# Four-pass output projection, half of the sample attention beside projections, plain first products and paired scores in a two-layer encoder step

## The chip, the cores and the metric

The kernel runs on one core of a Trainium2 chip, in one launch. The metric is the time of one execution on the device in microseconds. The engines are TensorE (matmuls, in the profile PE, its weight loads PEld), VectorE (DVE), ScalarE (ACT), GpSimd (POOL), and SyncE (SP), which issues most of the transfers.

## The reference

One inference step of two layers, d_model 1024, on 512 prompt tokens (one sequence) and 128 sample tokens (8 sequences of 16 new tokens, each with 512 cached keys and values).

- Layer 0: RMSNorm; a projection into mixer A (8 heads of 64, stick-breaking attention, strictly causal) and mixer B (gated linear attention, 4 heads); both outputs side by side through one output projection; residual.
- Layer 1: RMSNorm; mixer C, 16 heads of 64, softmax over 64-token chunks and the eight chunks before, with a learned bias by distance; output projection; residual.
- After each mixer RMSNorm and a SwiGLU FFN (hidden 2816), residual; a last RMSNorm.

```python
xp = xp + _ab_merge(oa, ob, r, norm_gla_g[i], w_out_ab[i])      # cat(oa, ob) @ w_out
...
xp = xp + (oc.reshape(Bp, Tp, C_WIDTH) @ w_out_c[i])
...
def _swiglu(h, wg, wu, wd):
    return (jax.nn.silu(h @ wg) * (h @ wu)) @ wd
```

Outputs are the normed tokens of both groups and the new keys, values and states.

## The kernel before

All 640 tokens are five blocks of 128 (four prompt blocks, one sample block). Every fp32 weight and activation that goes through a large matmul is split into a high and a low fp32r part (`split`: a ScalarE cast, L273, and a VectorE subtraction, L274), and each product is three matmuls (high-high, high-low, low-high). Weights come through `load_raw` (L267) on SyncE's queue into two buffers.

Order. The kernel is written against a tile framework that places instructions by a simulated timeline: an instruction goes when its inputs and buffers are there, lowest priority number first. Program order gives the number unless `priority(...)` sets one; the mixers' attention has large negative numbers and so is put in as soon as it can go, with projections filling in. Each engine, and each queue of transfers, then runs its own list in order.

Layer 0 (to about 447 us): `ORDER` lists the projections (V values, P query/key pair, G, K, R for mixer B, M its recurrence). `proj_ws` (L288 to L290) keeps the weight stationary, 320 tokens at a time; `proj_as2` (L337 to L340) gives values. After each pair `attend_prompt` runs the two heads of the pair: for each query block b and each head, three matmuls of contraction length 64 (rows 0 to 63 for head 0, 64 to 127 for head 1) put scores into a bank of PSUM (`za`), L436 to L438; `weights` turns them into weights (stick-breaking L403 to L411, softmax L418 to L423); transposes (L444) go back into the same bank, copies to SBUF follow (L447, L449), and the value products (L455) land in head 0's bank.

`attend_sample` does one of the eight sample sequences with all 8 heads of a half (a step): it loads the values (`vr`, 1 MB, L481, two buffers that it shares with the prompt's value tiles) and the keys (`kr`, four of 256 KB, L486), transposes the keys (L489), makes scores (L496), weights, their transposes (L508, L510), value products (L517) and a last transpose (L521). Mixer A has 8 steps, mixer C 16 (two halves).

`mixer_end` closes a mixer. It splits the outputs into `oH` and `oL` (L538, L539), issues all sample steps, then `out_prompt` (L561 to L563; four stretches of 256 output columns over the four prompt blocks, with the norm of each block in the last stretch; `WHEN` gives their place among the sample's priorities), and at the end `out_sample` (L579 to L581), which loads and splits the weight again for the sample block and normalises it.

FFN (`ffn`): the token operand is cut into quadrants b11, b12, b21, b22 (rows of d_model by 320-token halves), and a pair of 128-column weight blocks is multiplied by it with seven products instead of eight (`fast_pair`, L653 to L655) of sums and differences; the weight sums are made by POOL (L659), the token combinations t1 to t4 by VectorE (L621, split by L612 and L613), all at the start of the FFN in `operand`. A down projection (`proj_as`, L307 to L309) follows for each group of hidden blocks (`GROUPS`).

PSUM has eight banks: three for projections (`pp`), and in the mixers `BANKS = ((3, 2), (4, 1))`, that is `za` and `zb` with 3 and 2 in layer 0, 4 and 1 in layer 1; in the FFN all five are one pool.

Of the kernel before, what the change touches and what calls it, by code (L numbers as in the profile page):

```python
# [8 lines left out]
F32 = mybir.dt.float32  # L9
# [31 lines left out]
NGT = 6  # L41
NHL = 4
TAIL = 4
ORDER = "V0 P0 G0 P1 K0 V1 M0 P2 K1 R0 M1 R2 P3 R1 R3"
MPRI = 50000
WHEN = ((20, 20, 20, 20), (4, 8, 12, 15))
BANKS = ((3, 2), (4, 1))
KTA = "bbbb"
KTC = "baba"
# [6 lines left out]
def kernel(  # L56
# [16 lines left out]
    @contextmanager  # L73
    def mixer_pools(na, nb):

        with tc.tile_pool(name="mix", bufs=1, reuse_waits="tile") as m:
            pools["stage"] = m
            with tc.tile_pool(name="pza", bufs=na, space=PSUM, reuse_waits="tile") as a:
                with tc.tile_pool(name="pzb", bufs=nb, space=PSUM, reuse_waits="tile") as b:
                    banks.update(za=a, zb=b)  # L80
                    yield

    @contextmanager
    def ffn_pools():
        with tc.tile_pool(name="ffn", bufs=1, reuse_waits="tile") as m:
            pools["stage"] = m
            with tc.tile_pool(name="pf", bufs=5, space=PSUM, reuse_waits="tile") as a:
                banks.update(za=a, zb=a)
# [13 lines left out]
    qk = tagged("qk", NQK)  # L102
# [13 lines left out]
    def za(shape, name="za"):  # L116
        return banks["za"].tile(shape, F32, tag="za", name=name)
# [115 lines left out]
    def norm_block(xt, gi, hT, b, sb=None, bank=None):  # L233
        r = rstd_of(xt, sb)
        for i in range(2):
            tp = (bank or za)([P, 4, P], "tp")
# [59 lines left out]
    def proj_as(l, W, c0, n, lhs, evac, tail=1):  # L296
# [3 lines left out]
        ps = [pp([P, n], "pn") for _ in range(3)] + [za([P, n], "pn") for _ in range(2)]  # L300
# [73 lines left out]
    def evac_k(dst, kfd, kout_p, kout_s, hp):  # L374

        def f(ps):
# [8 lines left out]
            with priority(2 * FIRST):  # L385
                tp = zb([P, 4, P], "ktp")
# [3 lines left out]
                tp2 = zb([P, P], "ktp2")  # L390
# [35 lines left out]
    def attend_prompt(qT, kT, v, c0, odst, weights, mask):  # L426


        for b in range(4):
            n = (b + 1) * P  # L430
            bs = slice(b * P, n)
            wTs, zs = [], []
            for h in range(2):
                z = za([P, 512], "z")
                r = slice(64 * h, 64 * h + 64)
                MM(z[:, :n], lhsT=qT[r, 0, bs], rhs=kT[r, 0, :n], start=True, stop=False)  # L436
                MM(z[:, :n], lhsT=qT[r, 0, bs], rhs=kT[r, 1, :n], start=False, stop=False)
                MM(z[:, :n], lhsT=qT[r, 1, bs], rhs=kT[r, 0, :n], start=False, stop=not mask)  # L438
                if mask:
                    MM(z[:, bs], lhsT=identb, rhs=mask_a, start=False, stop=True)  # L440
                w = weights(h, n, z[:, :n])
                wT = vr_([P, b + 1, P], "wT")
                for j in range(b + 1):
                    nc.tensor.transpose(z[:, j * P:(j + 1) * P], w[:, j * P:(j + 1) * P], ident)  # L444
                zv = z[:, :n].rearrange("p (j t) -> p j t", t=P)
                if h == 0:
                    nc.scalar.copy(wT, zv)  # L447
# [720 lines left out]
```

## Time and profile before

| | |
|---|---|
| median of 3 runs | 1823.07 us (1819.52 to 1823.08) |
| profiled execution | 1823.8 us, span of its instructions 1822.1 us |
| TensorE busy | 1732.9 us (95%), mean granted clock 0.969 |
| VectorE, ScalarE, GpSimd busy | 1142.8, 833.8, 327.7 us |
| HBM | 175.75 MB read, 14.29 MB written |

A matmul's row in the time order gives its start and its own time; matmuls overlap, so the cost of one is the distance between starts. Rows by tile give smallest, median and largest time in ns and the starts of the first and the last. The granted clock (PEclk) is the share of full speed that TensorE was allowed.

### The profile page before, as it was taken

The page shows a single profiled execution, that of the slowest core. Times are in us where ns is not written, and L with a number is a line of the kernel's source. Part 1 is how long each engine was busy: PE and PEld are TensorE (multiplying, and loading weights), DVE is VectorE, ACT ScalarE, POOL GpSimd, SP SyncE. Part 2 cuts the span into 40 slices and gives each one's busy share as a digit, 9 for nine tenths or more (in the row PEclk, how much of TensorE's full clock was granted, in tenths as well). Part 3 has the DMA queues.
Part 4 walks back from the last instruction along what each step waited for, and adds up shares of the span by engine and source line. Part 5 has one row for each costly group of instructions (what it writes and reads, how often), then busy time and mean ns, then how long its engine had stood idle before and what let it go on. Part 6 is the DMA issues. An engine that isn't in the chain of part 4 may idle for free.

```text
span 1822.1 us, 31879 instructions
## 1 busy us (share of the span) xinstructions
PE 1732.9 (95%) x12504; PEld 1550.1 (85%) x12504; DVE 1142.8 (63%) x2285; ACT 833.8 (46%) x1837; POOL 327.7 (18%) x355
## 2 busy tenths in 40 slices
PE   8999998998899999999799999999878999999997
PEld 7898986976898989989698888888757989999896
DVE  5466576767964846747635554665658747658475
ACT  6453444556642534525424333444545525435253
POOL 2000000002513413222200000000104314133130
PEclk9998997998999999999799999999988999999999
DMA  5311222573222232221342223257862222312212
GB/s 141 94 56 47 66 83 95 179 255 105 70 93 70 75 100 63 100 74 66 110 128 77 80 89 95 85 178 263 278 214 65 81 81 72 103 58 93 93 59 81
DMA packets 157430, 192.10 MB, mean 105 GB/s; under 512 B 13232, under 2 KB 109504, under 8 KB 157280
## 3 DMA queue, kind: packets, MB, share of 16 engines
q1 hardware_dynamic: 153696, 178.40, 30.4%
q0 software_dynamic: 3584, 11.67, 2.0%
q8 instruction: 98, 1.61, 0.4%
q14 instruction: 52, 0.43, 0.1%
HBM read 175.75 MB, written 14.29 MB: 104 GB/s over the span
## 4 chain that ended last, share of the span: by engine, by line
PE 80%; DVE 12%; DMA 4%; ACT 2%; issue 2%; SPq 0%; DVEq 0%; ACTq 0%
PE pn L307 6%; PE pn L309 5%; PE pn L308 5%; PE pw L288 5%; PE pw L289 5%; PE pw L290 5%; DVE wl L274 4%; PE px L653 3%; PE px L654 3%; PE px L655 3%; PE z L455 3%; PE py L655 3%; DMA kr<-in_cache_c_k_dram 2%; PE pm L337 2%; PE py L653 2%; PE py L654 2%
## 5 line engine op out<-in xcount | busy, mean ns | idle before, releaser
L274 DVE TENSOR_TENSOR wl<-raw,wh 128x512 fp32r<-128x512 f32 (+1 forms) x350 | 279.3, 807 | 220.8 <-ACT wh L273 218.7
L273 ACT CAST wh<-raw 128x512 fp32r<-128x512 f32 (+1 forms) x350 | 215.4, 618 | 347.3 <-PE pn L309 162.6
L659 POOL TENSOR_TENSOR sw<-raw 128x512 f32<-128x512 f32 x88 | 121.6, 1386 | 498.9 <-DMA raw<-in_w_ffn_gate_dram 292.9
L273 ACT CAST wh<-sw 128x512 fp32r<-128x512 f32 x176 | 109.3, 621 | 177.8 <-PE px L654 78.2
L274 DVE TENSOR_TENSOR wl<-sw,wh 128x512 fp32r<-128x512 f32 x176 | 139.7, 798 | 60.3 <-ACT wh L273 49.1
L308 PE MATMUL pn<-wl,gT 128*128 128x512 f32 x440 | 172.7, 393 | 0.0
L309 PE MATMUL pn<-wh,gT 128*128 128x512 f32 x440 | 170.7, 392 | 0.0
L307 PE MATMUL pn<-wh,gT 128*128 128x512 f32 x440 | 168.8, 394 | 0.0
L655 PE MATMUL py<-xb,wl 128*128 128x320 f32 x352 | 113.1, 321 | 8.4 <-DVE wl L274 8.2
L653 PE MATMUL py<-xb,wh 128*128 128x320 f32 x352 | 111.4, 316 | 6.1 <-ACT wh L273 4.6
L654 PE MATMUL pq<-xt,wh 128*128 128x320 f32 x352 | 109.1, 310 | 2.9 <-DVE xt L613 2.7
L654 PE MATMUL px<-xt,wh 128*128 128x320 f32 x352 | 109.7, 312 | 1.6 <-DVE xt L613 1.6
L654 PE MATMUL py<-xb,wh 128*128 128x320 f32 x352 | 110.7, 314 | 0.0
L653 PE MATMUL px<-xt,wh 128*128 128x320 f32 x352 | 109.5, 311 | 0.0
L655 PE MATMUL px<-xt,wl 128*128 128x320 f32 x352 | 109.4, 311 | 0.0
L653 PE MATMUL pq<-xt,wh 128*128 128x320 f32 x352 | 109.1, 310 | 0.1
L655 PE MATMUL pq<-xt,wl 128*128 128x320 f32 x352 | 108.6, 309 | 0.0
L309 PEld LDWEIGHTS pn<-wh,gT 128*128 128x128 f32 x440 | 83.5, 190 | 17.4
L308 PEld LDWEIGHTS pn<-wl,gT 128*128 128x128 f32 x440 | 83.6, 190 | 17.2
L307 PEld LDWEIGHTS pn<-wh,gT 128*128 128x128 f32 x440 | 83.4, 190 | 16.8
L288 PE MATMUL pw<-hTa,wh 128*128 128x320 f32 (+1 forms) x272 | 89.5, 329 | 0.0
L290 PE MATMUL pw<-hTa,wl 128*128 128x320 f32 (+1 forms) x272 | 88.7, 326 | 0.0
(331 smaller groups left out, 4778.3 us busy)
## 6 DMA issues: line engine op xcount, KB each, us to landing
raw<-in_w_ffn_gate_dram SPq DMA_DIRECT2D x44, 512.0 KB, 4.1
raw<-in_w_ffn_up_dram SPq DMA_DIRECT2D x44, 512.0 KB, 3.7
raw<-in_w_ffn_down_dram SPq DMA_DIRECT2D x44, 512.0 KB, 3.3
kr<-in_cache_c_k_dram SPq DMA_DIRECT2D x64, 256.0 KB, 4.8
vr<-in_cache_c_v_dram SPq DMA_DIRECT2D x16, 1024.0 KB, 6.7
raw<-in_w_in_ab_dram SPq DMA_DIRECT2D x24, 512.0 KB, 3.8
raw<-in_w_qkv_c_dram SPq DMA_DIRECT2D x24, 512.0 KB, 3.8
vr<-in_cache_a_v_dram SPq DMA_DIRECT2D x8, 1024.0 KB, 5.5
```

Source lines behind the costliest of these rows:

```text
L273: nc.scalar.copy(H, rawv)
L274: nc.vector.tensor_sub(L, rawv, H.bitcast(F32))
L288: MM(ps[i], lhsT=H[:, k % 4, :], rhs=hT[k][:, 0, s], start=(k == 0), stop=False)
L289: MM(ps[i], lhsT=H[:, k % 4, :], rhs=hT[k][:, 1, s], start=False, stop=False)
L290: MM(ps[i], lhsT=L[:, k % 4, :], rhs=hT[k][:, 0, s], start=False, stop=(k == 7))
L307: MM(ps[b], lhsT=lhs[k][:, 0, bs], rhs=H, start=(k == 0), stop=False)
L308: MM(ps[b], lhsT=lhs[k][:, 0, bs], rhs=L, start=False, stop=False)
L309: MM(ps[b], lhsT=lhs[k][:, 1, bs], rhs=H, start=False, stop=(k == K - 1))
L653: MM(ps, lhsT=H[:, k, :], rhs=X[x][0][k], start=(first and k == 0), stop=False, **f)
L654: MM(ps, lhsT=H[:, k, :], rhs=X[x][1][k], start=False, stop=False, **f)
L655: MM(ps, lhsT=L[:, k, :], rhs=X[x][0][k], start=False, stop=(k == 3), **f)
L659: nc.gpsimd.tensor_tensor(t, a, b, op=op)
```

## The change

Four things, and what they need:

1. `attend_prompt` puts both heads' scores in one tile of two banks (`zz`, one buffer) and issues the six matmuls with the heads in turn; weights are transposed into another bank (`zt`: one buffer in layer 0, two in layer 1), and the value products land in head 1's transpose bank. `zb` has two and one. Key transposes, norms and sample steps take their banks from `zt`, `zb` and `zz`.
2. `out_prompt` and `out_sample` give way to `out_pass`: all five blocks, one half of the 8 input chunks (`kh`) by one half of the output columns (`half`), 512 columns a matmul, added to the residual rows after each pass. A mixer ends with four passes, mixer A with kh 1 (mixer B's outputs) first, mixer C with kh 0 first.
3. Mixer C's sample steps of half 0 are issued two at a time after the attention of pairs 4 to 7, with priorities between them; those of half 1 in `mixer_end`. Mixer A's are in `mixer_end`, four before the first pass and four after.
4. In the FFN the first weight pair is multiplied with eight plain products; the combinations t1 to t4 are written after the first products of the next two weight pairs.

The residual rows move into the large tile pool (18 buffers), query and key tiles into the mixers' pool, some FFN operands into the gate pool (9 buffers, 6 before).

```diff
+BANKS = ((1, 2), (2, 1))
...
+    def zz(name="zz"):
+        t = banks["zz"].tile([P, 2, 512], F32, tag="zz", name=name)
+        return [t[:, 0, :], t[:, 1, :]]
...
+            zs = zz("z")
+            for i, j in ((0, 0), (0, 1), (1, 0)):
+                for h in range(2):
+                    r = slice(64 * h, 64 * h + 64)
+                    MM(zs[h][:, :n], lhsT=qT[r, i, bs], rhs=kT[r, j, :n], start=(i + j == 0),
+                       stop=(i == 1 and not mask))
...
+            ws_ = [weights(h, n, zs[h][:, :n]) for h in range(2)]
+            wTs, ts = [], []
+            for h, w in enumerate(ws_):
+                t = zt([P, 512], "wtp")
...
-            o = zs[0][:, :P]
+            o = ts[1][:, :P]
...
+    def out_pass(W, kh, half, x, done=None):
+        HL = []
+        for k0 in (4 * kh, 4 * kh + 2):
+            raw = load_raw(W[k0 * P:(k0 + 2) * P, 512 * half:512 * half + 512], 2, 512)
+            for i in range(2):
+                HL.append(split(raw[:, i:i + 1, :], 1, 512))
+        for b in range(NB):
+            bs = slice(b * P, (b + 1) * P)
+            ps = pp([P, 512], "po")
+            for i in range(4):
...
+                MM(ps, lhsT=oHc, rhs=H, start=(i == 0), stop=False)
+                MM(ps, lhsT=oHc, rhs=L, start=False, stop=False)
+                MM(ps, lhsT=oLc, rhs=H, start=False, stop=(i == 3))
+            nc.vector.tensor_add(x[b][half], x[b][half], ps)
+            if done is not None:
+                done(b)
...
+        for st in sample[:4]:
+            st()
+        halves(k0)
+        x = [load_x(xsrc(b)) for b in range(NB)]
+        out_pass(W, k0, 0, x)
+        for st in sample[4:]:
+            st()
+        out_pass(W, k0, 1, x)
+        halves(1 - k0)
+        out_pass(W, 1 - k0, 0, x)
+        out_pass(W, 1 - k0, 1, x, lambda b: norm_block(x[b], gi, hT, b))
...
+        def plain():
+            HL = []
+            def part(n):
+                if n == 0:
+                    HL.extend([split(A[m][k], 4, P) for k in range(2)] for m in range(2))
+                for m in range(2):
+                    ps = zb([P, 320], "pb")
+                    for k in range(2):
+                        product(ps, None, (("b11", "b21"), ("b12", "b22"))[n][k], k == 0, HL[m][k])
+                    out(m, n, ps, None)
+            return part
...
+                    part = whole()
+                    block("b11")
+                    block("b21")
+                    part(0)
+                    block("b12", gt_)
+                    block("b22")
+                    part(1)
+                    mats[1][0]()
+                    mats[2][0]()
+                    comb("t3", "b22", "b12")
+                    block("t3")
+                    comb("t1", "b12", "b11")
+                    comb("t2", "b22", "t1")
+                    block("t2")
+                    block("t1")
+                    comb("t4", "b21", "t2")
+                    block("t4", gt_)
+                    continue
...
+    def c_steps(half):
...
+            if half == 0:
+                z.append(zt([P, 512], "zs"))
+            elif not z:
+                z.extend(zz("zs"))
+            p = FIRST + 200000 + (40000 + 5000 * b + 5500 if half == 0 else 90000 + 1000 * b)
...
+            with priority(p):
+                attend_sample(cache_c_k, cache_c_v, b, cs, qbd[half], zn, vt4[:, cs],
...
+                              oS[:, 4 * half:4 * half + 4, :], z.pop(0), "bbbb" if half == 0 else "baba")
...
+        for p in range(p0, p0 + 4):
+            if p > p0:
+                c_attend(p, *c_pair(p))
+            for st in steps[2 * (p - p0):2 * (p - p0) + 2]:
+                st()
+        steps = c_steps(half)
...
-    xt = mixer_end(w_out_c[0], oT, oS, lambda b: xd[b], 3, hT, lambda: [c_sample(h) for h in range(2)],
-                   [FIRST + 299500 + 1000 * t for t in WHEN[1]])
+    xt = mixer_end(w_out_c[0], oT, oS, lambda b: xd[b], 3, hT, steps, 0)
```

More of the change, by code (lines that the diff above doesn't have):

```diff
@@ L471, in new_key_scores, with attend_sample @@
         return zn
-    def attend_sample(ck, cv, b, cs, qbd, zn, vnew, weights, oS, kttp):
+    def attend_sample(ck, cv, b, cs, qbd, zn, vnew, weights, oS, z, kttp):
         def rows(src):
@@ new lines, in mixer_end, with halves @@
+    def mixer_end(W, oT, oS, xsrc, gi, hT, sample, k0):
+        for half in (oH, oL):
+            half[:] = [None] * 4
+        def halves(kh):
+            for i in (2 * kh, 2 * kh + 1):
+                oH[i], oL[i] = [t5([P, 2, NT], "oHL", F32R) for _ in range(2)]
+                out_split(oT[i], i, slice(0, SEQ))
+                out_split(oS[:, 2 * i:2 * i + 2, :], i, slice(SEQ, NT))
+        for st in sample[:4]:
[9 more added lines that the diff above has]
+        out_pass(W, 1 - k0, 1, x, lambda b: norm_block(x[b], gi, hT, b))
+        return x
@@ L603, in operand, with comb @@
     def operand(fT):
         n1, n2 = slice(0, 320), slice(320, NT)
-        out = {}
-        def block(nm, srcs):
+        out, t = {}, {}
+        t["b11"] = [fT[kp][:, :, n1] for kp in range(2)]
+        t["b21"] = [fT[2 + kp][:, :, n1] for kp in range(2)]
+        t["b12"] = [fT[kp][:, :, n2] for kp in range(2)]
+        t["b22"] = [fT[2 + kp][:, :, n2] for kp in range(2)]
+        def comb(nm, a, b):
+            t[nm] = []
+            for kp in range(2):
+                x = ws([P, 2, 320], "xs")
+                nc.vector.tensor_sub(x, t[a][kp], t[b][kp])
+                t[nm].append(x)
@@ L695, in tail @@
             out(1, 0, st["Q"], st["U"])
-        return head, body, tail
+        return head, body, tail, plain
     def ffn(l, xt, fT, after):
-        X = operand(fT)
+        X, comb, block = operand(fT)
         c0, silu = 0, []
@@ L703, in ffn @@
             for c in range(c0, c0 + G, 2):
[L704 removed]
+                gt = [gt_([P, 2, NT], "gT", F32R) for _ in range(2)]
                 gT += gt
@@ L726, in ffn @@
                     mats.append(fast_pair(w[l], c * P, X, o))
-            for i, (head, body, tail) in enumerate(mats):
-                if i == 0 or not (gi == 0 and i == 1):
+            for i, (head, body, tail, whole) in enumerate(mats):
+                if gi == 0 and i == 0:
+                    part = whole()
[16 more added lines that the diff above has]
+                    continue
+                if gi or i > 2:
                     head()
-                if gi == 0 and i == 0:
-                    mats[1][0]()
-                if i:
+                if i > (gi == 0):
                     mats[i - 1][2]()
```

222 lines of the change are left out of this document (73 added, 149 removed).

## The prediction

> **What bounds the kernel now.** I read the page's totals first, then the busy time of every engine in stretches of my choosing, then TensorE's instructions in order of time where a term needs a price, then the tables by tile for first and last starts.
>
> ```profile
> span 1822.1 us, 31879 instructions
> PE 1732.9 (95%) x12504; PEld 1550.1 (85%) x12504; DVE 1142.8 (63%) x2285; ACT 833.8 (46%) x1837; POOL 327.7 (18%) x355
> ```
>
> TensorE is busy for 95% of the span and no other engine is above 63%. What that is made of differs by stage:
>
> ```profile
> core 0: us, PE busy (x) PEld busy (x) DVE busy (x) ACT busy (x) POOL busy (x), PEclk, DMA share, GB/s
> 100.00:310.00 210.00, 208.44 (x1442) 181.50 (x1441) 133.66 (x269) 92.53 (x208) 7.15 (x12) 0.94 0.21 63
> 331.70:447.10 115.40, 103.04 (x1127) 88.34 (x1125) 79.31 (x157) 71.25 (x153) 11.37 (x29) 0.96 0.58 197
> 447.00:480.00 33.00, 28.21 (x154) 25.98 (x154) 31.34 (x45) 22.18 (x44) 19.91 (x11) 0.84 0.16 49
> 920.00:1170.00 250.00, 250.00 (x1720) 216.56 (x1720) 130.87 (x414) 93.64 (x244) 13.29 (x25) 1.00 0.29 88
> 1169.70:1369.50 199.80, 176.57 (x2236) 144.64 (x2234) 115.02 (x323) 96.29 (x228) 16.61 (x56) 0.96 0.67 224
> 1208.00:1340.00 132.00, 117.41 (x1747) 100.17 (x1740) 75.84 (x215) 68.04 (x161) 11.98 (x49) 0.99 0.81 270
> 1369.50:1400.00 30.50, 24.68 (x123) 23.34 (x124) 27.66 (x40) 17.41 (x33) 11.12 (x8) 0.78 0.17 53
> ```
>
> Beside projections (100 to 310, 920 to 1170) TensorE has no idle time and the DMA engines stand at 0.21 to 0.29. From 1208 to 1340 it is the other way round: DMA 0.81 at 270 GB/s, TensorE 15 us idle. The two starts of an FFN (447, 1369) have TensorE idle, VectorE nearly full, and a granted clock of 0.84 and 0.78. So instructions taken from TensorE pay in full beside projections; elsewhere it is a chain or a transfer that pays. The stages' ends are these:
>
> ```profile
> L290 PE MATMUL pw<-hTa,wl x272: 302/309/712, 48.9 to 331.7; 128*128 128x320 f32 x128, 128*16 128x320 f32 x8
> L290 PE MATMUL pw<-hTc,wl x256: 302/309/417, 936.3 to 1169.7; 128*128 128x320 f32 x128
> L653 PE MATMUL py<-xb,wh x352: 303/309/636, 447.1 to 1779.3; 128*128 128x320 f32 x176
> ```
> ```profile
> L517 PE MATMUL zs<-vt4c,wT x128: 272/273/421, 1223.9 to 1351.3; 128*32 128x128 f32 x128
> L517 PE MATMUL zs<-vt,wT x64: 272/273/421, 353.5 to 422.9; 128*32 128x128 f32 x64
> ```
>
> Projections end at 331.7 and 1169.7. The samples' last value products run to 422.9 (8 steps, 69.4/7 = 9.9 us apart) and 1351.3 (16 steps, 127.4/15 = 8.5 us apart). The first FFN product comes at 447.1.
>
> **The change. Part 1: two heads' scores in a double bank.** One head's scores at 256 keys:
>
> ```profile
> 1022.51 0.31 PE L289 MATMUL pw<-hTc,wh 128*128 128x320 f32 x1
> 1022.65 0.31 PE L290 MATMUL pw<-hTc,wl 128*128 128x320 f32 x1
> 1022.89 0.38 PE L436 MATMUL z<-kTc,qTc 64*128 64x256 f32 x1
> 1023.11 0.28 PE L437 MATMUL z<-kTc,qTc 64*128 64x256 f32 x1
> 1023.23 0.28 PE L438 MATMUL z<-kTc,qTc 64*128 64x256 f32 x1
> 1023.44 0.42 PE L288 MATMUL pw<-hTc,wh 128*128 128x320 f32 x1
> 1023.69 0.31 PE L289 MATMUL pw<-hTc,wh 128*128 128x320 f32 x1
> ```
> ```profile
> 562.13 0.39 PE L307 MATMUL pn<-wh,gT 128*128 128x512 f32 x1
> 562.36 0.39 PE L308 MATMUL pn<-wl,gT 128*128 128x512 f32 x1
> 562.59 0.39 PE L309 MATMUL pn<-wh,gT 128*128 128x512 f32 x1
> ```
>
> Start to start a matmul costs 0.146 us at 320 columns and 0.228 at 512 (0.46 for two); the line through both gives 0.119 at 256, 0.173 at 384 and 0.065 at 128. From 1022.65 to 1023.69 are 1.04 us, of which two 320s are 0.29: the group costs 0.75, of it 3 x 0.119 columns and 0.39 for entering and leaving the half-height form. Over the four blocks a head costs 3 x (0.065+0.119+0.173+0.228) + 4 x 0.39 = 3.3 us, and a pair 6.6. Afterwards both heads stand in one group, rows 0-63 and 64-127 in turn. No row shows this form; the bounds are the quarter-array products against the half-width ones:
>
> ```profile
> 233.06 1.10 PE L924 MATMUL kv<-vb,kdn 64*64 64x128 f32 x32
> ```
> ```profile
> 1018.03 1.09 PE L455 MATMUL z<-wT,vc 128*64 128x128 f32 x14
> ```
>
> Less the 0.27 us that the last one takes to run out, 32 records in 1.10 us are 27 ns each, 14 in 1.09 are 63: halving the rows as well doubles the rate, so the two halves run side by side. Full overlap gives 3.3 us a pair, a saving of 3.3; none saves only a switch, 1.6; were each change of half to cost 0.2, the pair would lose 2.4. I take 3.0, beside the kv row. Twelve pairs, all where TensorE is full: 12 us in mixer A, 24 in mixer C.
> The Trainium skill (TensorE: Matmul & The Clock Gate, Part 3, Measured speedup) gives four row tiles at once 3.07x, not 4x. At that efficiency two tiles would give 1.54x, a pair 3.8 us, and the saving would be 34 us over twelve pairs rather than the 40 of full overlap; my 36 stands between.
>
> Transposes move from the score bank to another, one bank in A and two in C; they and the value products keep their counts.
>
> **Part 2: four passes.** Per mixer now 384 matmuls of 256 columns and 48 of 512: 384 x 0.119 + 48 x 0.228 = 46 + 11 = 57 us. After: 240 of 512, 54.6. The columns are equal; 2.4 us go. Loads of the weight fall from 24 to 8, splits from 32 to 16; those of the sample's own projection are the ones that stood in a chain. But the last sample value product will be followed by two passes over all blocks, 2 x 60 x 0.228 = 27.3 us, with normalisation of each block behind its last matmul. From the last projection matmul to the FFN's first it takes this now:
>
> ```profile
> 1366.62 0.40 PE L581 MATMUL ps<-wh,oHL 128*128 128x512 f32 x1
> 1369.54 0.41 PE L653 MATMUL py<-xb,wh 128*128 128x320 f32 x1 [2.52 <-ACT wh L273]
> ```
>
> I take these 3 us again and 1.5 for splitting the last outputs: 32 us after the last sample value product, against 24 (422.9 to 447.1) and 18 (1351.3 to 1369.5) now. The passes are full of work where the old tail idled, but the tail itself gets longer.
> Residual rows will land in other tiles, loaded beside a pass; cover gone, one landing, 4 us. Moved tile pools, norm weights and gate buffers issue the same instructions: nothing, or at most 5 us should the two gate tiles kept for the FFN delay a group.
>
> **Part 3: half of the sample beside projections (mixer C).** A step's TensorE cost:
>
> ```profile
> 341.36 0.60 PE L489 MATMUL kttp<-ident,kr 128*128 128x128 f32 x4
> 341.89 0.65 PE L496 MATMUL zs<-kt,qbda 128*32 128x128 f32 x16
> 342.46 0.66 PE L489 MATMUL kttp<-ident,kr 128*128 128x128 f32 x4
> 342.87 0.36 PE L561 MATMUL po<-wh,oHL 128*128 128x256 f32 x1
> ```
> ```profile
> 352.58 1.08 PE L517 MATMUL zs<-vr,wTs 128*32 128x128 f32 x32
> 353.48 0.40 PE L517 MATMUL zs<-vt,wT 128*32 128x128 f32 x8
> 353.81 0.39 PE L561 MATMUL po<-wh,oHL 128*128 128x256 f32 x1
> ```
>
> Half the key side takes 1.51, the values 1.23, six more transposes 0.11 each (four in 0.60, the last 0.27), switches some 0.5 (two of 0.2 to 0.4): 5.4 us. Eight steps are issued along pairs 4 to 7; I let six finish there. They add 32 us where TensorE is full, and pairs 0 to 6 give 21 back: projections end at 1181. The loads (2 MB a step, on SP) find the DMA engines at 0.29; the small copies and clears on POOL queue behind its output issues and the bias clear. A pair here lasts 14 us of projections, some 4.5 of attention and two steps of 5.4, so 15 us a step; the key side, through one bank for its transposes, takes four times 0.7 and a copy of about 0.7, some 6, and the attention chain below another 6 to 8. It just fits, and three pairs give six steps.
>
> ```profile
> L418 DVE CUSTOM_DVE_ANT_0 s<-z,bias 128x128 f32<-128x128 f32 (+3 forms) x64 | 31.2, 490 | 20.2 <-PE z L438 19.2 <-issue 0.6
> L421 ACT ACTIVATE s<-s,m 128x128 f32<-128x128 f32 (+3 forms) x64 | 36.0, 562 | 68.5 <-DVE m L420 68.5
> ```
>
> What remains after 1181: by TensorE the last pair and a half 14, ten steps 54, output 55, norms 4 = 127 us; by the chain four blocks of attention 20 (an estimate: ten steps of about 0.5 us each, as in the two rows above), two late steps 20, seven intervals of 8.5 = 60, then 32: 132 us. The two are nearly equal and share queues, so I add 12: 1181 + 132 + 12 = 1325. Now: 1369.5. **Mixer C: -44 us**, of it 24 by part 1.
>
> **Mixer A.** Projections end 12 earlier, at 320, and the first value product follows at 341. The steps have only two passes as filler (27 us, not 46), so I take 8.7 us an interval instead of 9.9: 341 + 61 + 32 = 434, against 447. **Mixer A: -13**. By TensorE's work alone (43 + 55 + 4 after 320) it would be 422 + 3, -22.
>
> **Part 4: plain products first.** From 447 to 480 stand 146 products and 8 transposes, 22 us of work in 33; from 1369.5 to 1400 115 and 8, 18 in 30.5: 23.5 us lost, waiting for the combined operands and at the lower clock. Now 8 plain products need only uncombined blocks (the first four only three normed token blocks), 14 us, then four heads, 7 us, while the combinations are made. That is 12 matmuls more, 1.75 us each time; three splits and four POOL sums fewer. I leave 4 us lost per start: **-12**. All gone would be -20; cover no better than now +3.5.
>
> **Sum.** This execution took 1823.8 us (span 1822.1 and 1.7 around it), 0.7 above the median of 1823.07. 1823.8 - 44 - 13 - 12 = 1754.8; with 2 of the 5 us at most for the gate tiles, **1757**.
>
> **Rivals.**
>
> ```profile
> L407 DVE TENSOR_TENSOR_SCAN l<-l 128x128 f32<-128x128 f32 (+4 forms) x40 | 36.2, 905 | 0.5
> ```
> ```profile
> SPq L481 <- PE zs L517: 34.8, 19, 5.0
> ```
>
> *The double bank holds the scores back.* There is one, where there were three or four banks; it is free only when both heads have been read. In C that is two reads of 0.49 us, little against 7.8 us of stage per block (250/32); in A the bank stays taken from the first of the stick-breaking steps to the last but one, the scan of 0.9 us and five of about 0.5, the second head's behind the first's: some 6 us of 13 (210/16). If the attention chain and not TensorE then sets the pace, part 1's 36 us do not come: 1793. The Trainium skill (TensorEngine Tiling (Array Packing), Performance Considerations) warns of just this: tiling speeds up TensorE and not the emptying of PSUM. The rows above leave room, so 0.15.
>
> *The half sample is not beside the projections.* The order is a planner's; the value loads have one free buffer of two while the other holds this half's values, and POOL's small steps may be late. If the steps run after the projections after all, mixer C keeps only its 24: 1777, chance 0.12.
>
> *Slower: a value load stops SP's queue.* With one buffer the load of step b+1 waits for step b's products, and the weight loads behind it on SP wait too. Two loaded weights cover 2 x 48 x 0.146 = 14 us of projection; beyond that TensorE stands. To lose all 67 us, eight waits must each exceed 14 + 8.4 = 22 us; at 25 us the time is 1757 + 8 x 11 = 1845. Waits for that buffer now are at most 5.0. Chance 0.09, a third of it with waits that only eat the gain up.
>
> **Chances.** Forecast (1725 to 1775) 0.58, bank 0.15, late steps 0.12, SP 0.09; 0.06 for better than 1725 (TensorE's own sums in both mixers, 1181 + 127 + 3 in C, and clean FFN starts: 22 + 58 + 20 = 100, 1724). 0.2% is 3.6 us, about what this kernel's measurement can tell. Faster 0.91, same 0.03, slower 0.06. Range 1720 to 1800, from the better bounds to just past the bank rival.
>
> **What would show it.** Right: six score matmuls per block within 1.1 us at 512 keys; value loads of the C cache beside projections with DMA above 0.4 there; no long waits for cache keys; first FFN products about 434 and 1306 (1369.5 - 44 - 13 - 6) with the clock at 1.0 soon after. Wrong: TensorE idle beside projections, waiting for weights, or scores waiting for reads; sample steps bunched after the last projection; the passes waiting for the sample's last step.

## The result, and the profile after

The changed kernel takes 1878.8 us (median) against 1821.3 for the kernel before, a ratio of 1.032 (95% interval 1.029 to 1.035): 57 us slower, where 66 less were forecast. Its profiled execution has a span of 1872.1 us, 50 more than the one shown of before. From the page:

```profile
span 1872.1 us, 30990 instructions
PE 1718.5 (92%) x12144; PEld 1510.5 (81%) x12144; DVE 1131.7 (60%) x2247; ACT 815.8 (44%) x1803; POOL 311.9 (17%) x347
```

TensorE does 14 us less work than before and its idle time has grown from 89 to 154 us. Where, the stretches tell (columns as in the prediction: busy time and count of each engine, granted clock, DMA share, GB/s):

```profile
331.00:443.70 112.70, 80.12 (x810) 55.41 (x810) 44.93 (x75) 42.80 (x77) 3.49 (x22) 0.77 0.42 141
443.70:463.40 19.70, 18.70 (x72) 15.10 (x73) 9.97 (x20) 7.14 (x19) 5.92 (x5) 0.85 0.18 54
463.40:480.90 17.50, 8.70 (x43) 5.90 (x41) 15.79 (x42) 14.45 (x44) 4.25 (x5) 0.69 0.18 60
936.00:1181.70 245.70, 245.70 (x2030) 222.42 (x2029) 134.52 (x420) 96.20 (x258) 14.83 (x31) 1.00 0.38 117
1254.00:1389.70 135.70, 103.47 (x1101) 72.45 (x1097) 49.04 (x120) 39.78 (x81) 4.43 (x28) 0.81 0.45 151
1409.20:1426.30 17.10, 8.13 (x42) 6.24 (x41) 14.66 (x42) 14.70 (x44) 4.52 (x4) 0.68 0.18 61
```

Beside mixer C's projections (936 to 1181.7) TensorE is still full. In the samples' stretches (331 to 443.7, 1254 to 1389.7) no engine is: TensorE stands still for 32 us in each, the DMA engines run at 0.42 and 0.45, VectorE and ScalarE are busy for 29 to 40% of the time. Where nothing is full, a chain of dependent instructions is the first thing to look for. The stages' ends by tile (first and last start after "median/max"; the last two rows are the second half of mixer C alone, here and in the kernel before):

```profile
L293 PE MATMUL pw<-hTa,wl x272: 302/309/468, 51.8 to 291.1; 128*128 128x320 f32 x128, 128*16 128x320 f32 x8
L524 PE MATMUL zs<-vt,wT x64: 272/345/421, 353.2 to 442.8; 128*32 128x128 f32 x64
L634 PE MATMUL pb<-xb,wh x64: 307/309/615, 480.9 to 1441.3; 128*128 128x320 f32 x64
L293 PE MATMUL pw<-hTc,wl x256: 302/309/417, 966.3 to 1181.7; 128*128 128x320 f32 x128
L524 PE MATMUL zs<-vt4c,wT x128: 272/273/421, 1142.0 to 1388.8; 128*32 128x128 f32 x128
L524 PE MATMUL zs<-vt4c,wT x64: 272/420/421, 1284.9 to 1388.8; 128*32 128x128 f32 x64
L517 PE MATMUL zs<-vt4c,wT x64: 272/273/421, 1301.7 to 1351.3; 128*32 128x128 f32 x64
```

Mixer A's steps: 89.6/7 = 12.8 us apart (9.9 before). In mixer C the eight steps of the second half take 103.9 us from first to last, 14.8 apart; before, the second half's were 7.1 apart (49.6/7), and 8.5 over all sixteen. The first of these seven intervals is of another kind than the rest: from 1284.9 to 1313.8 TensorE is busy for 28.54 of 28.90 us, since 100 matmuls of output passes stand between the two steps (about 23 us at 0.228 each). The last six take 75.0 us, 12.5 each, with TensorE busy for 48.96 us. The tail, from the last value product to the first FFN product, takes 38.1 us (24.2 before) and, to 1426.3, 37.5 us (18.2). The first FFN starts 33.7 us later than before and lasts 3.8 less; mixer C takes 26.8 more from the first FFN's end to the second's start; the second FFN lasts 6.8 less. Together 49.9, the difference of the spans.

The reason for the 12.5 stands in TensorE's and VectorE's rows in order of time, at the seam of two steps of the second half, where one hands the tile on to the next:

```profile
1314.39 0.29 DVE L527 COPY osb<-zs 128x128 f32<-128x128 f32 x1 [1.18 <-PE zs L524]
1314.73 0.33 PE L528 MATMUL zs<-ident,osb 128*128 128x128 f32 x1 [0.48 <-DVE osb L527]
1315.10 0.46 DVE L532 COPY oSc<-zs 64x64 f32<-64x64 f32 x2 [0.42 <-PE zs L528]
1315.70 0.65 PE L503 MATMUL zs<-kt,qbdc 128*32 128x128 f32 x16 [0.64 <-DVE oSc L532]
```

The last read of one step's tile (L532) ends at 1315.56, and only then do the scores of the next step begin (L503, released by it). All six seams from here on are like this: the scores begin 0.05 or 0.06 us after the last read where the step takes the other bank of the same tile, and 0.15 us after it where the tile is taken anew. In this stretch two steps are never under way together. Before they were: scores of a third step stand at 341.89 and the first step's value products only at 352.58 and 353.48 (rows in the prediction).

Mixer A shows the same with a comparison built in, since its steps take the two halves of the double tile and one bank more in turn. From value product to value product it takes 18.1, 11.0, 8.7, 16.5, 11.1, 8.7 and 15.4 us: the three long intervals are the three at which a step takes the second half of a double tile whose first half the step before it is using.

The waits of 1254 to 1389.7 (total, times, longest) show the cost on ScalarE:

```profile
ACT kt L501 <- PE zs L503: 37.6, 7, 12.7
```

Seven times ScalarE waits, up to 12.7 us, to copy the next step's transposed keys: their buffers are held until the late scores have used them.

The paired scores themselves do what they should. At 512 keys, between projections:

```profile
999.70 0.31 PE L293 MATMUL pw<-hTc,wl 128*128 128x320 f32 x1
999.93 0.96 PE L441 MATMUL z<-kTc,qTc 64*128 64x512 f32 x6
1000.83 0.42 PE L291 MATMUL pw<-hTc,wh 128*128 128x320 f32 x1
1001.08 0.31 PE L292 MATMUL pw<-hTc,wh 128*128 128x320 f32 x1
```

From 999.70 to 1001.08 are 1.38 us, 0.29 of it two projection matmuls: 1.09 for both heads. One head alone cost as much before (1037.97 to 1039.35):

```profile
1037.97 0.31 PE L288 MATMUL pw<-hTc,wh 128*128 128x320 f32 x1
1038.21 0.49 PE L436 MATMUL z<-kTc,qTc 64*128 64x512 f32 x1
...
1039.10 0.42 PE L289 MATMUL pw<-hTc,wh 128*128 128x320 f32 x1
1039.35 0.31 PE L290 MATMUL pw<-hTc,wl 128*128 128x320 f32 x1
```

In mixer A the prompt's own blocks meet the double tile too. There the last read of a block's scores (L413) comes at the end of a long chain of stick-breaking steps:

```profile
238.69 0.96 PE L441 MATMUL z<-kT,qT 64*128 64x512 f32 x6
253.38 0.68 DVE L413 TENSOR_TENSOR l<-z,l 128x512 f32<-128x512 f32 x1
257.08 0.33 PE L441 MATMUL z<-kT,qT 64*128 64x128 f32 x2
```

In the last eight blocks the tile is held for 10 to 18 us and blocks follow 12 to 18 us apart. Projections end 40 us earlier than before (291.1 against 331.7), but the prompt's last value products stand at 331.7, against 328.9.

The tail in mixer A, from the last output matmul to the FFN's first product (rows between left out):

```profile
463.42 0.39 PE L563 MATMUL po<-wh,oHL 128*128 128x512 f32 x1
...
480.10 1.12 PE L243 MATMUL tp<-ident,h 128*128 128x128 f32 x4 [3.07 <-DVE fT L249]
480.86 0.61 PE L634 MATMUL pb<-xb,wh 128*128 128x320 f32 x1
481.27 0.47 PE L635 MATMUL pb<-xb,wh 128*128 128x320 f32 x1
481.54 0.47 PE L636 MATMUL pb<-xb,wl 128*128 128x320 f32 x1
```

Five normalisations stand in this gap, VectorE and ScalarE nearly full (15.8 and 14.5 of 17.5 us), and the first product comes after the last block's transposes.

### The profile page after: what moved, and what is told of

Its sections match the earlier page's. It is cut to its first block, busy times and chain, and to the rows that moved or that the text cites. A ratio compares the mean times of both kernels' runs of the same rounds, so it can differ in the third digit from the quotient of the medians.

```text
span 1872.1 us, 30990 instructions
## 1 busy us (share of the span) xinstructions
PE 1718.5 (92%) x12144; PEld 1510.5 (81%) x12144; DVE 1131.7 (60%) x2247; ACT 815.8 (44%) x1803; POOL 311.9 (17%) x347
## 4 chain that ended last, share of the span: by engine, by line
PE 79%; DVE 14%; ACT 4%; issue 2%; DMA 1%; POOL 0%; DVEq 0%; SPq 0%; ACTq 0%; POOLq 0%
PE pn L310 5%; PE pn L312 5%; PE pn L311 5%; PE pw L291 4%; PE pw L292 4%; PE pw L293 4%; DVE wl L277 3%; PE px L635 3%; PE px L634 3%; PE px L636 3%; PE py L636 2%; PE kttp L496 2%; PE pm L340 2%; PE pm L343 2%; PE pm L342 2%
## 5 line engine op out<-in xcount | busy, mean ns | idle before, releaser
L277 DVE TENSOR_TENSOR wl<-raw,wh 128x512 fp32r<-128x512 f32 (+1 forms) x352 | 274.0, 789 | 226.7 <-ACT wh L276 224.9
L654 POOL TENSOR_TENSOR sw<-raw 128x512 f32<-128x512 f32 x84 | 117.5, 1403 | 542.7 <-DMA raw<-in_w_ffn_gate_dram 267.7
L276 ACT CAST wh<-sw 128x512 fp32r<-128x512 f32 x168 | 104.2, 621 | 158.9 <-PE px L635 66.5
L636 PE MATMUL py<-xb,wl 128*128 128x320 f32 x336 | 106.3, 316 | 11.2 <-DVE wl L277 11.2
L636 PE MATMUL pq<-xt,wl 128*128 128x320 f32 x336 | 103.7, 310 | 1.8 <-DVE wl L277 1.8
L635 PE MATMUL px<-xt,wh 128*128 128x320 f32 x336 | 103.8, 309 | 0.0
L634 PE MATMUL px<-xt,wh 128*128 128x320 f32 x336 | 103.8, 309 | 0.0
L635 PE MATMUL py<-xb,wh 128*128 128x320 f32 x336 | 103.8, 309 | 0.0
L636 PE MATMUL px<-xt,wl 128*128 128x320 f32 x336 | 103.8, 309 | 0.0
L635 PE MATMUL pq<-xt,wh 128*128 128x320 f32 x336 | 103.8, 309 | 0.0
L634 PE MATMUL pq<-xt,wh 128*128 128x320 f32 x336 | 103.8, 309 | 0.0
L634 PE MATMUL py<-xb,wh 128*128 128x320 f32 x336 | 103.8, 309 | 0.0
L311 PEld LDWEIGHTS pn<-wl,gT 128*128 128x128 f32 x440 | 83.3, 189 | 17.1
L312 PEld LDWEIGHTS pn<-wh,gT 128*128 128x128 f32 x440 | 83.2, 189 | 17.1
L291 PE MATMUL pw<-hTa,wh 128*128 128x320 f32 (+1 forms) x272 | 89.2, 328 | 3.4 <-DVE er L890 2.6
L292 PE MATMUL pw<-hTa,wh 128*128 128x320 f32 (+1 forms) x272 | 87.7, 322 | 0.0
```

What stands on the lines that cost most here:

```text
L276: nc.scalar.copy(H, rawv)
L277: nc.vector.tensor_sub(L, rawv, H.bitcast(F32))
L291: MM(ps[i], lhsT=H[:, k % 4, :], rhs=hT[k][:, 0, s], start=(k == 0), stop=False)
L292: MM(ps[i], lhsT=H[:, k % 4, :], rhs=hT[k][:, 1, s], start=False, stop=False)
L311: MM(ps[b], lhsT=lhs[k][:, 0, bs], rhs=L, start=False, stop=False)
L312: MM(ps[b], lhsT=lhs[k][:, 1, bs], rhs=H, start=False, stop=(k == K - 1))
```

## The experiments

All kernels against the kernel before in the same session (1817 to 1821 us); a difference of a few us between two experiments is no more than that spread. Theory 1 is that the sample's steps are held back by the tile of two banks, which is taken and released as one, with the longer tail as its second half. Rival A blames the tail alone, rival B the half sample beside projections.

**Two single-bank tiles in the changed kernel.**

```diff
-  tc.tile_pool(name="pzz", bufs=1, ...)
+  tc.tile_pool(name="pzz", bufs=2, ...)
-  t = banks["zz"].tile([P, 2, 512], ...); return [t[:, 0, :], t[:, 1, :]]
+  return [banks["zz"].tile([P, 512], ...) for _ in range(2)]
```

> The changed kernel with its double bank made of two tiles of one bank each; the scores of a pair still go out as one group, and nothing else differs. Theory 1 (the two-bank tile is taken and released as one, so a sample step's scores wait for the last read of the step before): the interval between the samples' last value products falls from 12.5 to some 9 us in mixer C (half 1) and from 12.8 to some 10 in mixer A, 7 x 3.5 + 7 x 2.8 = 44 us less, 1835 us. Rival A (the tail of two passes and five normalisations behind the sample makes the loss): the intervals may shrink, but the FFN starts move by less than 10 us, 1870 us or more. Rival B (the half sample beside projections with its shared value buffer makes the loss): half 1 starts no earlier than 1284 us and its intervals stay above 12 us, 1875 to 1882 us.

Measured: 1831.3 us, ratio 1.007 (1.004 to 1.009); 47.5 us less than the changed kernel, by an edit that leaves the number of instructions of every engine as it was. By tile for the second half of mixer C, and in order of time:

```profile
L523 PE MATMUL zs<-vt4c,wT x64: 272/273/421, 1271.5 to 1341.1; 128*32 128x128 f32 x64
```
```profile
1296.40 0.60 PE L514 MATMUL zs<-ident,zsb 128*128 128x128 f32 x4
...
1299.54 0.43 PE L502 MATMUL zs<-kt,qbdc 128*32 128x128 f32 x8
...
1300.51 0.33 PE L516 MATMUL zs<-ident,wn 128*128 128x128 f32 x1
```

The second half's steps are 9.9 us apart (69.4/7) where they were 14.8, and mixer A's 9.5 where they were 12.8. The 9.9 is a mean of two kinds again: 17.2 and 17.9 us beside output passes, with TensorE busy for 34.20 of 35.10 us, and 6.9 us for the last five, where the changed kernel has 12.5. Between the weight transposes of one step (L514, L516) stand scores of the next (L502): two steps are under way. The tails stay at 37 and 39 us. Theory 1 holds; rivals A and B, as causes of the main loss, fall. The prompt's pairs have single banks here as well; a later run takes the two apart.

**Part 1 undone in the changed kernel** (the function of the prompt's scores and the banks as before; parts 2, 3 and 4 stay).

```diff
-BANKS = ((1, 2), (2, 1))
+BANKS = ((3, 2), (4, 1))
-  z.extend(zz("zs") + [zt([P, 512], "zs")])
+  z.append(zt([P, 512], "zs"))
```

> The changed kernel with the paired scores undone: each head's scores in a bank of its own, 3 and 1 banks more to choose from for scores and sample steps, as in the kernel before; four passes, half sample and plain products stay. Theory 1: sample steps come back to 9 to 10 us apart in both mixers (-44 us), and the pairs beside projections cost some 2 to 3 us each again (12 pairs, +24 to +36): 1860 to 1870 us, with the last projections later and the first FFN products earlier. Rival A: the paired scores are pure gain and the tail is the loss: 1878 + 30 = 1905 us or more. Rival B: intervals stay above 12 us, 1900 us.

Measured: 1849.9 us, ratio 1.016 (1.011 to 1.020), 10 us below what theory 1 expected. As it came, part 1 cost 29 us; with single-bank tiles it brings 18.6. Parts 2 to 4 alone are 31 us slower than before.

**Part 1 alone on the kernel before**, double bank for the sample's steps too.

> The kernel before with the paired scores alone (the sample's steps get the double bank and, in mixer A, one bank more, as in the changed kernel). Theory 1: projections end some 12 us (A) and 24 us (C) earlier, but the sample's steps come 12 to 13 us apart instead of 9.9 and 8.5: 7 x 2.9 - 12 = +8 in A, 15 x 4 - 24 = +36 in C, together 1821 + 44 = 1865 us. Rivals A and B (part 1 is not to blame): 1821 - 36 = 1785 us, with steps no further apart than before.

Measured: 1907.0 us, ratio 1.049 (1.045 to 1.052), worse than expected and worse than the whole change. The sixteen steps of mixer C, by tile:

```profile
L527 PE MATMUL zs<-vt4c,wT x128: 272/417/421, 1224.5 to 1438.1; 128*32 128x128 f32 x128
```

They are 213.6/15 = 14.2 us apart, not the 12.5 that I had carried over, and all sixteen wait, where the changed kernel has eight. The mean granted clock of the span is 0.929, 0.969 before.

**Part 4 alone on the kernel before** (operands, products and FFN loop as in the changed kernel).

> The kernel before with the plain products first in the FFN alone. Both FFNs took 10.6 us less in the changed kernel (455.2 against 459.0 and 434.0 against 440.8, first product to last). If that is part 4's doing: 1811 us. Rival (it is the later start, with more of the operands ready, and not the order of products): within 3 us of 1821.

Measured: 1825.1 us, ratio 1.004 (1.002 to 1.006): neither forecast, it costs 6 us. In its profile the FFNs are 2.9 and 4.3 us shorter, but the first product comes 30.0 and 25.3 us behind the sample's last value product (419.1 to 449.1, 1347.5 to 1372.8), 24.2 and 18.2 before. The 6 us are a difference of medians: the two profiled executions have spans of 1821.1 and 1822.1 us, so the profile shows the two effects and not their sum.

**Part 2 alone on the kernel before.**

```diff
-  sample(); out_prompt(W, xt, gi, hT, when); ...; out_sample(W, xt[4], gi, hT)
+  sample(); halves(k0); out_pass(W, k0, 0, x); out_pass(W, k0, 1, x)
+  halves(1 - k0); out_pass(W, 1 - k0, 0, x)
+  out_pass(W, 1 - k0, 1, x, lambda b: norm_block(x[b], gi, hT, b))
```

> The kernel before with the four passes alone: its own banks, its own order of products, all sample steps at the mixer's end. Theory 1, second half (what is left of the loss once the two-bank tile is gone is the tail: two passes and five normalisations behind the sample's last value product, 37.5 us with two single-bank tiles, against 24 and 17.4 before): steps stay 8.5 to 10 us apart, the tails become 36 to 38 us, +13 in mixer A and +20 in mixer C, 1850 to 1855 us. Rival (the tail is that long only because scores and half sample are elsewhere): tails as before, 1821 - 3 to 1821 + 5 us.

Measured: 1843.2 us, ratio 1.014 (1.011 to 1.018), 24 us slower. The tails, from the last value product's stage to the first FFN product:

```profile
427.50:458.10 30.60, 23.91 (x105) 19.57 (x106) 18.77 (x48) 16.94 (x50) 9.03 (x8) 0.83 0.29 86
1356.00:1388.70 32.70, 25.78 (x105) 20.82 (x106) 19.57 (x50) 17.03 (x50) 8.71 (x8) 0.76 0.31 97
```

From the last value product itself they are 31.5 and 33.5 us, less than the 36 to 38 expected here and just the 32 of the prediction. The 38 of the changed kernel are 6 longer, which is what part 4 alone adds to a tail.

**Part 3 undone, with two single-bank tiles.**

```diff
-  for st in steps[2 * (p - p0):2 * (p - p0) + 2]: st()
+  for st in c_steps(0): st()      # after the last pair
```

> The changed kernel with two single-bank tiles and with the half sample undone: all sixteen steps of mixer C at its end, none beside projections. If the half sample is worth what the prediction gave it (-20 us in mixer C without the scores' 24): 1831 + 20 = 1851 us. If, as the kernel with single banks and with part 1 undone suggest, the loads' rate sets the pace wherever the steps stand: 1825 to 1837 us, projections ending some 13 us earlier, sixteen steps 8.5 to 9 us apart. If it costs (rival B): 1815 us or less.

Measured: 1834.8 us, ratio 1.008 (1.006 to 1.010). The half sample beside projections is worth 3.5 us by the medians, not 20, and the two ratios' intervals overlap. Undone, projections of mixer C end at 1163.4 instead of 1172.2, sixteen steps follow 10.0 us apart, and the last value product comes at 1343.0 against 1341.1. The prompt's own attention shows where the gain goes: without the half sample its last value products stand at 1181.8, with it at 1242.0. With sample steps between its last pairs, the prompt's attention ends 70 us behind the projections instead of 18.

**Pairs in ordinary banks, on the kernel before.**

```diff
+  pair = [za([P, 512], "z") for _ in range(2)]
+  for i, j in ((0, 0), (0, 1), (1, 0)):
+      for h in range(2): MM(pair[h][:, :n], ...)
```

> The kernel before with one thing of part 1: the score matmuls of two heads go out in turn, into two ordinary banks of the shared pool, and transposes go back into those banks as before. Theory 1: the pairing is worth 24 us in mixer C (what two single-bank tiles against none of part 1 gave there) and 0 to 12 in mixer A, and the sample's steps keep their banks: 1785 to 1797 us. Rival (with two banks held by a pair, a third or a fourth is too few for the sample's steps): 1815 us or more, with steps further apart than 8.5 and 9.9 us.

Measured: 1819.4 us, ratio 0.999 (0.998 to 1.001), no change. Neither theory was tested, since the pairs did not come about; in order of time:

```profile
1000.39 0.96 PE L437 MATMUL z<-kTc,qTc 64*128 64x512 f32 x3
1001.28 0.42 PE L289 MATMUL pw<-hTc,wh 128*128 128x320 f32 x1
```

Three matmuls of one head, then projections: with a bank for each head the planner sent one head ahead of the other. Three take 0.96 us of busy time here, six 0.96 in the changed kernel. The tile of two banks has a use: in the changed kernel, which has it, both heads go out in turn.

**The sample's rows put behind, with two single-bank tiles.**

```diff
-  out_pass(W, 1 - k0, 0, x)
-  out_pass(W, 1 - k0, 1, x, lambda b: norm_block(...))
+  out_pass(W, 1 - k0, 0, x, range(4))
+  HL = out_pass(W, 1 - k0, 1, x, range(4), nb)
+  halves(1 - k0, p=False)                       # split of the last sample rows
+  out_pass(W, 1 - k0, 1, x, [4], None, HL)
+  out_pass(W, 1 - k0, 0, x, [4], nb)
```

> The changed kernel with two single-bank tiles, and with the sample's rows of the last two passes put behind: both passes over the four prompt blocks, with their normalisations, come first in the order, then the sample's block of the second half with the weights still held, then that of the first half with its weights loaded and split again (4 loads and 16 splits more). Theory 1: the tail falls from 37.5 us to some 15 to 18 in each mixer (split 1.5, two times 12 matmuls 5.5, a split between 3, one normalisation 5), -20 each: 1790 us. Rival (the prompt's passes and normalisations slow the sample's steps as much as they shorten the tail): 1820 us or more, with steps 12 us apart.

Measured: 1822.5 us, ratio 1.001 (1.000 to 1.003). The tails fall to 26.4 and 28.1 us, but only 9 us of the 40 come: in mixer C the steps of the second half are now 11.4 apart (1262.2 to 1342.2). The rival's forecast is the nearer one.

**The same with part 4 undone.**

> The kernel with two single-bank tiles and the sample's rows put behind (1822 us), with the order of FFN products of the kernel before. If part 4 costs here what it cost alone (6 us): 1817 us. If it is worth the 3 to 6 us by which both FFNs were shorter in the traces: 1826 us.

Measured: 1809.5 us, ratio 0.994 (0.992 to 0.995): part 4 costs 13 us here. First the end of mixer A with part 4, then without:

```profile
448.81 1.94 PE L242 MATMUL tp<-ident,h 128*128 128x128 f32 x8 [7.24 <-DVE h L240]
450.40 0.62 PE L640 MATMUL pb<-xb,wh 128*128 128x320 f32 x1
```
```profile
438.37 0.39 PE L562 MATMUL po<-wh,oHL 128*128 128x512 f32 x1
440.77 0.56 PE L651 MATMUL py<-xb,wh 128*128 128x320 f32 x2 [2.02 <-ACT xb L610]
```

With part 4 the first product stands in TensorE's order behind the sample block's transposes, which wait 7.2 us for its normalisation; its sum needs two split blocks of the operand. In the old order the first product needs one, and starts 2.4 us after the last output matmul, before the sample block is normalised. In the first FFN that head start is used up again (its last product starts at 904.3 with part 4 and at 905.0 without); the gain appears at the second one, reached 13 us earlier (1357.5 against 1370.3), 8.6 of them in the tail (19.5 us against 28.1).

**Double bank for the prompt, single banks for the sample, in the changed kernel.**

```diff
+  def single_banks():          # called where the mixer's prompt attention has been written out
+      banks["inner"].close()
+      banks["zz"] = banks["inner"].enter_context(tc.tile_pool(name="pzs", bufs=2, ...))
```

> The changed kernel with the double bank kept for the prompt's pairs alone; when a mixer's prompt attention is written out, its two banks become two single ones for the sample's steps. Against the kernel with two single-bank tiles throughout (1831 us) only the prompt's pairs differ: with single tiles the trace shows many pairs broken up (three matmuls of one head alone at 512 keys cost as much as six in turn, 1.1 us), here all go out in turn. If the pairing is what part 1 earned: some 10 broken pairs a mixer mended at up to 1 us each, 1820 us. If the double tile's hold on the prompt's own blocks costs as much (the prediction's bank rival): 1831 us or more.

Measured: 1829.4 us, ratio 1.004 (1.002 to 1.006). Against part 1 undone this is -20.5 us, the worth of the pairs in the changed kernel; against single tiles throughout it is 2 us less, within the spread of its runs. In mixer C whole pairs do shorten the way from the first projection to the next FFN, by 9 us (454.5 against 463.6). In mixer A the double bank's hold shows: the prompt's last value products come at 339.2, against 317.9 with single tiles. The first FFN product comes 4.8 us later there, no more than that mixer differs by from run to run, so what the hold costs in the end is not shown. It is not what the change lost 57 us by.

**All of it: swap of banks, sample's rows behind, old order of products.**

> All that the runs speak for: paired scores in the double bank for the prompt, single banks for the sample's steps, half sample beside projections, sample's rows of the last passes behind, order of FFN products of the kernel before. If the gains add (10 for unbroken pairs, 6 for the products): 1807 us, faster than both. If the sample's loads set the end of both mixers whatever TensorE saves: 1817 to 1822 us, the same as before.

Measured: 1800.9 us, ratio 0.989 (0.988 to 0.991), faster than both kernels. Its tails are 13.5 and 20.1 us long; by stretch, from shortly after the last value product on, columns as above:

```profile
426.00:437.80 11.80, 8.09 (x45) 6.15 (x43) 10.96 (x31) 10.00 (x32) 3.69 (x4) 1.00 0.31 88
1330.40:1348.60 18.20, 10.02 (x47) 6.90 (x46) 17.00 (x39) 13.39 (x41) 9.51 (x7) 0.87 0.54 155
```

**Part 1 alone with the swap, on the kernel before.**

> The kernel before with part 1 alone, as in the kernel at 1907 us, but with the double bank kept for the prompt's pairs and turned into two single banks for the sample's steps. Theory 1 says that all 88 us of loss of part 1 alone were the steps' hold on the double bank, and that the pairing itself is worth the 20.5 us between the changed kernel without part 1 (1849.9) and with the double bank kept for the prompt (1829.4): 1800 us, steps 8.5 to 10 us apart. Rival (before's mixer ends are set by the sample's loads, DMA 0.81 in mixer C, so earlier projections only wait): 1815 us or more.

Measured: 1809.7 us, ratio 0.994 (0.991 to 0.996), between the two forecasts. Against part 1 alone with the double bank for the steps this is 97 us less. By tile:

```profile
L306 PE MATMUL pw<-hTc,wl x256: 302/309/426, 936.9 to 1146.2; 128*128 128x320 f32 x128
L537 PE MATMUL zs<-vt4c,wT x128: 272/273/421, 1196.9 to 1335.0; 128*32 128x128 f32 x128
```

Mixer C begins at 906.9 here, so its projections end after 239.3 us, 263.3 before: 24 less. The sixteen steps begin 27 us earlier in the mixer but are 9.2 apart instead of 8.5, and 16 of the 24 arrive at the FFN. In mixer A nothing arrives (first FFN product at 448.5). Why 9.2, a seam in the kernel with two single-bank tiles shows, where two single banks serve the steps as well:

```profile
1311.11 0.46 DVE L531 COPY oSc<-zs 64x64 f32<-64x64 f32 x2 [3.79 <-PE zs L527]
1311.71 0.64 PE L502 MATMUL zs<-kt,qbdc 128*32 128x128 f32 x16 [0.30 <-DVE oSc L531]
```

The scores still follow the last read of an earlier step at once: now that of the step before the last. In this run's own trace twelve steps in a row begin 0.15 to 1.2 us after that read. Before the change there were four banks here, for scores, steps and half of the key transposes.

**A third bank for the steps of mixer C**, first in the kernel of part 1 alone with the swap.

```diff
-  z.extend(zs_pair())
+  z.extend(zs_pair() + [zt([P, 512], "zs")])
```

> The kernel with part 1 alone and the swap (1809.7 us), with one edit: the sample's steps of mixer C take a third bank in turn, one of the two that the transposes use. With two single banks every step's scores still begin 0.5 to 1.3 us after the last read of the step before the last. If the bank sets the 9.2 us between steps: 8.5 or less, and the 8 us of the pairs' gain that were lost in mixer C come back in part, 1802 to 1806 us. If the loads do (2 MB a step): 9.2 as before, 1808 to 1812 us.

Measured: 1786.9 us, ratio 0.983 (0.979 to 0.987): the fastest of all, 23 us less than with two banks (20 by the two ratios), more than expected. By tile:

```profile
L537 PE MATMUL zs<-vt4c,wT x128: 272/273/273, 1191.5 to 1314.7; 128*32 128x128 f32 x128
```
```profile
1190.00:1322.00 132.00, 116.74 (x1702) 95.19 (x1701) 76.99 (x215) 69.49 (x164) 10.35 (x47) 0.95 0.77 260
```

The steps are 8.2 us apart (123.2/15), DMA engines and rate are near what they were before (0.77 and 260 GB/s). Mixer C, from 901.5 to the FFN's first product at 1331.9, takes 430.4 us, 32.7 less than before; mixer A, in which nothing was edited, gives 5.5 (441.6), where the same lines gave nothing in the run above. What is under 10 us in one profile of mixer A should not be read as the edit's, so of the 23 us the trace shows 16.7, those of mixer C (447.1 with two banks), as the third bank's.

Then the same third bank in the kernel that had all parts.

> The kernel with all that the runs spoke for (1800.9 us), with the same third bank for the second half's steps of mixer C. If the bank sets the 11.7 us between them (1247.2 to 1328.5, seven intervals of 11.6): 10 us, 1790 to 1795 us. If the passes and loads do: 1799 to 1802 us.

Measured: 1798.0 us, ratio 0.988 (0.985 to 0.991), 3 us less. The second half's steps are 10.6 us apart (1252.8 to 1327.3): here the bank was not what set them. The same stretch by engine says what did:

```profile
1252.80:1303.00 50.20, 50.20 (x483) 38.40 (x471) 27.14 (x62) 19.15 (x38) 3.71 (x16) 1.00 0.69 234
1303.00:1327.30 24.30, 20.18 (x263) 15.76 (x266) 10.25 (x30) 8.63 (x23) 1.16 (x4) 0.96 0.31 104
```

Up to 1303 TensorE has no idle time at all, and 123 matmuls of output passes stand between the steps there, about 28 us of the 50 at 0.228 each. Parts 2 and 3, with the tail mended, leave the kernel 11 us slower than part 1 alone.

## Why the prediction was wrong, point by point

- **The failing step is the interval of the sample's steps:** "seven intervals of 8.5", 60 us in mixer C, and 8.7, 61 us in mixer A. Measured are 103.9 and 89.6, 72 us more, out of some 120 by which forecast and measurement differ. The prediction gave the double bank to the prompt's pairs in its sums and left out that the sample's steps take it too. There each seam costs the whole chain of scores, weights and products: 12.5 to 14.2 us a step. Two single banks take 47.5 us off. Of the 103.9 us one interval of 28.9 is not the bank's but the output passes'.
- **The bank rival** saw that a double bank is held until both heads have been read, but priced it on the prompt's blocks alone, as some 6 us of 13 in mixer A; there it is held for 10 to 18 us of 12 to 18. Of part 1's 12 us in mixer A little or nothing is seen: the two runs of part 1 alone with single banks for the steps reach the first FFN 1.4 us later and 5.5 us earlier than before, with nothing edited in that mixer between them. The rival was right in kind, and its 1793 us named only a small part of what the same tile costs the sample's steps.
- **Paired scores:** right in size where TensorE is full. A pair at 512 keys costs 1.09 us, one head cost that before; projections of mixer C fall by the 24 us forecast. Of the 36 forecast for part 1 alone, 30 are measured when mixer C's steps have three banks (the trace gives mixer C 32.7), 11 when they have two, and a loss of 88 when they have the double bank. The mixer's gain hung on a bank that the price list of part 1 did not name.
- **Four passes:** the 32 us tail was right for part 2 alone (31.5 and 33.5), the gain from passes that are full of work was not: 24 us slower alone. In the changed kernel the tail is 38.1 and 37.5 us, with errors of both signs: 72 of 120 matmuls were left behind the last value product (19.7 us, not 27.3), and from the last matmul to the first FFN product it took 17.4 and 17.1 us, not 3. The 3 us came from the row of a tail in which the prompt's blocks had long been normalised.
- **Half sample:** that projections end at 1181.7, where 1181 was forecast, is luck. Mixer C begins 30 us later than before (936.3 against 906.4), so its projections took 245 us, not the 275 of the forecast. Two steps of eight have their value products by then, not six; four steps at the forecast's 5.4 us are 22 of the 30. From there to the second half's first value product it took 103 us where 40 and the 12 of reserve stood. The DMA share beside the projections rises to 0.38 (above 0.4 forecast). With single-bank tiles the part is worth 3.5 us by the medians, not 20: the rival of late steps, at a chance of 0.12, came true for most of the steps.
- **Plain products:** both FFNs are shorter by 10.6 us together (12 forecast), but measured from the first product, which itself comes later: part 4 alone costs 6 us, and 13 once the tail is shorter. The prediction counted work and idle time behind the first product and not what stands ahead of it.
- **The value load on SP** did not happen in the form feared: TensorE is idle for 0 us from 936 to 1181.7.

So in the kernel with all parts and three banks it is passes in TensorE's order that space the second half's steps, as far as 1303; behind that TensorE is busy for 20.18 of 24.30 us. Open is whether another place for the passes would bring back the 11 us that parts 2 and 3 cost against part 1 alone, and what part 1 could gain in mixer A with a shorter hold. Neither was tried.

The Trainium skill (TensorE: Matmul & The Clock Gate, Part 1, What's actually happening) says that TensorE's clock is passed at half rate after an idle window and whole after a busy one. The rows fit that: the mean granted clock is 0.77 and 0.81 in the stages of waiting steps, 0.69 in the tail, and the first products of 320 columns behind it stand 0.27 us apart (481.27 to 481.54) against 0.146 in the full stages. So a chain costs a second time, in what follows it: in the passes behind mixer A's steps (443.70 to 463.40), with TensorE busy for 18.70 of 19.70 us, the clock is still 0.85.

## What to carry to other kernels

When a tile is made larger for one use, list every other user of that tile and price the seam at which each hands it on: what is allocated as one is waited for as one, even where two users touch different banks. Count a tail from the last product to the first of the next stage, normalisations and queue order included, and count a stage that "starts earlier" or "runs shorter" only by when the next one starts. And where an order comes from a planner, grouping instructions in the source does not group them on the engine: a shared buffer does.

## What the runs showed of the hardware

Two heads on the two halves of TensorE's rows run fully side by side: six matmuls of 512 columns in turn cost what three of one half do (0.96 us of busy time for either group, 1.09 with the switches), a speed-up of 2.0. I had taken somewhat less than that; the 1.54x that the prediction worked out from four row tiles does not carry over to two. The rest that surprised, the waits on a tile, is the program's, not the chip's.
